# Which engine issues a transformer layer's first loads: eight token tiles from ScalarE's DMA queue instead of SyncE's

## The chip, the cores and the metric

The kernel runs on one core of a Trainium2 chip. Its engines are TensorE (PE for matrix products, PEld for the loads of their stationary operand), VectorE (DVE), ScalarE (ACT), GpSimd (POOL) and SyncE (SP). Each takes the instructions of its own queue in order, and they meet through semaphores. SP and ACT can both issue DMAs; the transfers run on 16 DMA engines. The metric is the device time of one execution, in microseconds (us). A measurement is the median of several runs.

## The reference

One layer of a hybrid backbone over 1024 latent tokens of 1024 channels, with 256 context tokens, in float32. What the change touches is the very beginning: modulation vectors from `c`, and a modulated RMS norm of the tokens that goes into the input projection.

```python
mod_x = (jax.nn.silu(c) @ w_mod[i] + b_mod[i])[:, None, :]
mod_c = (jax.nn.silu(c_ctx) @ w_mod[i] + b_mod[i])[None, None, :]
sh1, sc1, g1, sh2, sc2, g2 = jnp.split(mod_x, 6, axis=-1)
h = modulate(rms_norm(x, norm1_g[i]), sh1, sc1)      # h * (1 + scale) + shift
hc = modulate(rms_norm(ctx, norm1_g[i]), csh1, csc1)
proj = h @ w_in[i]
...
# S5 scans in both directions, pooling mixer, gated sum, output projection, residual
h2 = modulate(rms_norm(x, norm2_g[i]), sh2, sc2)
x = x + g2 * swiglu(h2, w_ffn_in[i], w_ffn_out[i])
return rms_norm(x, final_norm_g)
```

## The kernel before

The program is written out as one long sequence, and each engine's order is the order of the source. All products are float32 accuracy from split operands: each operand is divided into a high and a low part (ACT copies the high part, DVE subtracts), and three products are summed. `startup` is the first of the phases that `run` calls (lines 339 to 373); input projection, S5 states, gates, branches and the two feed-forward products come behind it.

`startup` (lines 474 to 728) loads and prepares the tokens:

- The tokens come as eight tiles of 128 tokens by 1024 channels, 512 KB each (`load_x`, line 482). The source is an access pattern of 8 by 16 rows of 1024 floats; the target `x3` holds all eight tiles side by side.
- Modulation needs the product of silu(c) with 2048 columns of `w_mod`, in four pairs of columns kp = 0 to 3 (shift and scale, 256 each). For every kp two loads of four rows of blocks come in (`load_mod(kp, i)`, line 489; each i is two DMAs of 512 KB into a buffer `wm`, of which there are three). `mod_rows(kp)` (line 537) multiplies both halves on PE and lets ACT copy the result, `mrow`; `mod_cols` (548) turns it into columns, with `b_mod` and `norm1_g` added on DVE from `self.cols`.
- Eight slabs of `w_in` of 192 KB (`load_slab`, line 499, three buffers) are split on ACT and DVE (`split_slab`). `slab(k)` splits slab k and loads slab k + 3.
- Per tile: a sum of squares (`squares`, ACT, one of them on DVE), a reciprocal root on DVE (`rstds`), a scaling (`scale`, on DVE and ACT by turns). Per block of channels: four transposes on PE (`trans`), the modulation on ACT and DVE (`mod`), and the products with a slab (`mm(kt, q)`, nine matmuls).

The calls at lines 587 to 725 set the order by hand. On SP stand the rows of `c` and `c_ctx` (`load_small`, line 391), two loads of modulation columns (four DMAs), the rows of `b_mod` and `norm1_g`, four tiles, two slabs, four tiles, more columns and slabs. On ACT stand the small loads of the S5 parameters (`s5_load_a`, line 877: `nat` twice and `ldt`, which DVE copies into `nat` at line 885). `self.cols[:, 0:16]` is silu of c and c_ctx (`columns(0)`, line 434), which DVE copies into `ccols` (line 607), the stationary operand of `mod_rows`.

The framework gives every DMA of SP and of ACT one of eight counting semaphores, DMAHW0 to DMAHW7, by turns in the order of the program. The order rows further down name them as waits.

Of the kernel before, what the change touches and what calls it, by code (L numbers as in the profile page):

```python
# [235 lines left out]
class Kernel:  # L236
# [237 lines left out]
    def startup(self, hs):  # L474
        nc = self.nc
        st = ExitStack()
        sp = st.enter_context(self.pool("startup", side="right"))
        self.hp = hs.enter_context(self.pool("h"))
        self.h = [self.hp.tile([128, 8, 1024], F32R, name=f"h{i}") for i in range(2)]
        x3 = sp.tile([128, 8, 1024], F32, name="x3")  # L480

        def load_x(t):
            src = bass.AP(tensor=self.x.tensor, offset=self.x.offset + t * D,
                          ap=[[8 * D, 8], [64 * D, 16], [1, D]])
            nc.sync.dma_start(x3[:, t], src)

        wm = {}

        def load_mod(kp, i):

            wm[kp, i] = sp.tile([128, 4, 2, 256], F32, name="wm", bufs=3)
            for s in range(2):
                c = s * D + kp * 256
                nc.sync.dma_start(wm[kp, i][:, :, s], self.w_mod[0, i * 512:i * 512 + 512, c:c + 256].rearrange(
                    "(k p) m -> p k m", p=128))
# [90 lines left out]

        self.rows = {}
        self.load_small(sp, 0)
        load_mod(0, 0)
        load_mod(0, 1)  # L590
        self.load_small(sp, 1)
        for t in range(4):
            load_x(t)
        load_slab(0)
        load_slab(1)
        for t in range(4, 8):
            load_x(t)
# [2 lines left out]
        self.constants()  # L600
        nc.scalar.activation(self.cols[:, 0:1], self.sgn, AF.Silu)
        self.window_sizes(sp)
        self.s5_load_a(sp)
        self.columns(0)
        ccols = sp.tile([128, 8, 32], F32, name="ccols")
        nc.gpsimd.memset(ccols, 0.0)
# [1487 lines left out]
```

## Time and profile before

| | us |
|---|---|
| median of 3 runs | 1327.31 |
| lowest and highest | 1327.28, 1331.72 |
| the profiled execution | 1331.82 |
| its span, first to last instruction | 1330.0 |

| engine | busy us | share of the span |
|---|---|---|
| PE | 1250.9 | 94% |
| PEld | 1006.5 | 76% |
| DVE | 952.6 | 72% |
| ACT | 520.7 | 39% |
| POOL | 11.1 | 1% |

The mean granted TensorE clock over the span was 0.981. In the views, a time that stands first in a row is counted from the start of the span. A row of the timeline is: start, duration, engine, line, operation, output <- input, number of instructions, and in brackets the idle time of the engine before it with what ended it. "ACTq" and "SPq" are those engines' instruction queues, where DMA issues stand; the duration of an issue isn't that of the transfer. The chain of waits is followed back from the last instruction: each piece is either work or the time until something landed. Idle time of an engine that isn't the bottleneck costs nothing by itself.

### The profile page before, as it was taken

What the parts mean: (1) busy time and instruction counts of PE and PEld (TensorE: products, weight loads), DVE (VectorE), ACT (ScalarE), POOL (GpSimd) and SP (SyncE); (2) the same over time, 40 slices, a digit from 0 to 9 for tenths busy, and PEclk for the clock granted to TensorE, in tenths of its full rate; (3) what the DMA queues carried; (4) which work ended last, traced back from release to release, by engine and by line L of the source; (5) the groups of instructions that cost most, each with busy time, mean ns of one, the idle gap of its engine ahead of it and who ended that gap; (6) DMA issues with size and microseconds to landing.
All of it is one profiled execution on the core that took longest, in us unless ns stands there. A gap on an engine that the chain in (4) does not pass through costs nothing.

```text
span 1330.0 us, 16713 instructions
## 1 busy us (share of the span) xinstructions
PE 1250.9 (94%) x5811; PEld 1006.5 (76%) x5811; DVE 952.6 (72%) x1802; ACT 520.7 (39%) x939; POOL 11.1 (1%) x36
## 2 busy tenths in 40 slices
PE   4898979999969999999998999999999999999995
PEld 3676757778867788788876788888888888888884
DVE  4679984799705686865678886687778766578576
ACT  3575213652215432232454333333333345454343
POOL 3000000000000000000000000000000000000000
PEclk8899999999989999999998999999999999999998
DMA  6834469226376565653513643676666538776543
GB/s 202 218 128 150 155 204 313 97 85 217 112 204 239 194 216 184 223 174 106 198 44 110 218 131 100 141 236 221 223 200 210 170 132 317 275 227 192 180 138 127
DMA packets 196108, 239.79 MB, mean 180 GB/s; under 512 B 16608, under 2 KB 117560, under 8 KB 195512
## 3 DMA queue, kind: packets, MB, share of 16 engines
q1 hardware_dynamic: 188168, 223.45, 52.9%
q10 hardware_dynamic: 7856, 15.27, 3.0%
q8 instruction: 46, 0.75, 0.2%
q14 instruction: 38, 0.31, 0.1%
HBM read 168.67 MB, written 70.00 MB: 179 GB/s over the span
## 4 chain that ended last, share of the span: by engine, by line
PE 59%; DVE 19%; DMA 10%; ACT 6%; issue 4%; SPq 2%; ACTq 0%; DVEq 0%
PE ps L1721 10%; PE ps L1723 10%; PE ps L1722 10%; PE ps L1952 5%; PE ps L1953 5%; PE ps L1951 5%; PE ps L264 3%; PE ps L268 3%; PE ps L266 3%; DMA x<-in_x_dram 2%; PE ps L1565 2%; PE ps L1567 2%; PE ps L1566 2%; DVE wt L98 1%; DVE V L1260 1%
## 5 line engine op out<-in xcount | busy, mean ns | idle before, releaser
L1721 PE MATMUL ps<-a,wt 128*128 128x512 f32 x436 | 173.6, 398 | 4.5 <-ACT ld L1835 4.2
L1723 PE MATMUL ps<-a,wt 128*128 128x512 f32 x436 | 172.2, 395 | 0.3 <-DVE wt L124 0.3
L1722 PE MATMUL ps<-a,wt 128*128 128x512 f32 x436 | 171.5, 393 | 0.0
L124 DVE TENSOR_TENSOR a<-a,a 128x512 fp32r<-128x512 f32 x162 | 103.3, 685 | 30.9 <-ACT a L225 30.4
L1952 PE MATMUL ps<-a,a 128*128 128x512 f32 x308 | 122.0, 396 | 1.1 <-DVE a L124 1.1
L1951 PE MATMUL ps<-a,a 128*128 128x512 f32 x308 | 121.8, 396 | 0.0
L1953 PE MATMUL ps<-a,a 128*128 128x512 f32 x308 | 121.8, 396 | 0.0
L264 PE MATMUL ps<-h,wt 128*128 128x512 f32 x336 | 109.9, 408 | 6.9 <-ACT wt L97 6.4
L268 PE MATMUL ps<-h,wt 128*128 128x512 f32 x336 | 105.8, 397 | 2.2 <-DVE wt L98 1.9
L266 PE MATMUL ps<-h,wt 128*128 128x512 f32 x336 | 105.5, 396 | 0.0
L225 ACT ACTIVATE a<-a 128x512 fp32r<-128x512 f32 x154 | 87.7, 624 | 43.3 <-DVE a L124 13.2
L1721 PEld LDWEIGHTS ps<-a,wt 128*128 128x128 f32 x436 | 82.4, 189 | 23.2 <-ACT ld L1835 4.6
L1723 PEld LDWEIGHTS ps<-a,wt 128*128 128x128 f32 x436 | 82.4, 189 | 20.7 <-DVE wt L124 1.2
L1722 PEld LDWEIGHTS ps<-a,wt 128*128 128x128 f32 x436 | 82.5, 189 | 18.6
L1365 ACT ACTIVATE a<-ld 128x512 fp32r<-128x512 f32 x64 | 39.3, 629 | 129.1 <-DVE ld L1542 64.6
L264 PEld LDWEIGHTS ps<-h,wt 128*128 128x128 f32 x336 | 60.7, 192 | 22.1 <-ACT wt L97 7.9
L268 PEld LDWEIGHTS ps<-h,wt 128*128 128x128 f32 x336 | 61.4, 191 | 16.8 <-DVE wt L98 4.7
L266 PEld LDWEIGHTS ps<-h,wt 128*128 128x128 f32 x336 | 62.0, 191 | 12.6
L98 DVE TENSOR_TENSOR wt<-raw,wt 128x1024 fp32r<-128x1024 f32 (+1 forms) x42 | 39.8, 950 | 42.6 <-ACT wt L97 42.5
L1952 PEld LDWEIGHTS ps<-a,a 128*128 128x128 f32 x308 | 57.9, 188 | 15.8 <-DVE a L124 1.9
L1951 PEld LDWEIGHTS ps<-a,a 128*128 128x128 f32 x308 | 57.9, 188 | 13.9
L1953 PEld LDWEIGHTS ps<-a,a 128*128 128x128 f32 x308 | 57.9, 188 | 13.8
(335 smaller groups left out, 2445.1 us busy)
## 6 DMA issues: line engine op xcount, KB each, us to landing
raw<-in_w_ffn_in_dram SPq DMA_DIRECT2D x44, 512.0 KB
ld<-in_w_mod_dram SPq DMA_DIRECT2D x64, 256.0 KB
a<-in_w_ffn_out_dram SPq DMA_DIRECT2D x55, 256.0 KB
raw<-in_w_in_dram SPq DMA_DIRECT2D x10, 1024.0 KB
wm<-in_w_mod_dram SPq DMA_DIRECT2D x16, 512.0 KB
ld<-in_w_ffn_out_dram SPq DMA_DIRECT2D x22, 256.0 KB
x<-in_x_dram SPq DMA_DIRECT2D x8, 512.0 KB
ETd<-out ACTq DMA_DIRECT2D x16, 256.0 KB
```

What stands on the lines that cost most here:

```text
L98: nc.vector.tensor_tensor(lo, src, hi.bitcast(F32), op=OP.subtract)
L124: self.K.nc.vector.tensor_tensor(lo, self.src, hi.bitcast(F32), op=OP.subtract)
L225: K.nc.scalar.activation(hi, t, AF.Copy)
L264: nc.tensor.matmul(o, wh, ah, start=first, stop=False)
L266: nc.tensor.matmul(o, wh, al, start=False, stop=False)
L268: nc.tensor.matmul(o, wl, ah, start=False, stop=last)
L1721: nc.tensor.matmul(p, wh, ah, start=first and k == 0, stop=False, skip_group_check=on)
L1722: nc.tensor.matmul(p, wh, al, start=False, stop=False, skip_group_check=on)
L1723: nc.tensor.matmul(p, wl, ah, start=False, stop=last and k == 3, skip_group_check=on)
L1951: nc.tensor.matmul(p, ah[:, s], wh, start=first and i == 0, stop=False, skip_group_check=on)
L1952: nc.tensor.matmul(p, ah[:, s], wl, start=False, stop=False, skip_group_check=on)
L1953: nc.tensor.matmul(p, al[:, s], wh, start=False, stop=i == NB - 1, skip_group_check=on)
```

## The change

`load_x` issues its DMA from ACT, and `s5_load_a` is called before the tiles' loads instead of after `window_sizes`.

```diff
@@ -482,7 +482,7 @@
         def load_x(t):
             src = bass.AP(tensor=self.x.tensor, offset=self.x.offset + t * D,
                           ap=[[8 * D, 8], [64 * D, 16], [1, D]])
-            nc.sync.dma_start(x3[:, t], src)
+            nc.scalar.dma_start(x3[:, t], src)
@@ -586,6 +586,7 @@
         self.rows = {}
         self.load_small(sp, 0)
+        self.s5_load_a(sp)
         load_mod(0, 0)
         load_mod(0, 1)
         self.load_small(sp, 1)
@@ -600,7 +601,6 @@
         self.constants()
         nc.scalar.activation(self.cols[:, 0:1], self.sgn, AF.Silu)
         self.window_sizes(sp)
-        self.s5_load_a(sp)
         self.columns(0)
```

ACT's queue from its start, before, with the counters that a row waits for (nat and ldt are the S5 parameters, cols the Silu of c, mrow the modulation row, x3 the tiles):

```order
L601 ACT_TABLE_LOAD
L601 ACTIVATE cols_317<-sgn_311 128x1 [waits DVE_49]
L882 DMA nat_341<-in_s5_a_re_dram 64x2x64
L882 DMA nat_341<-in_s5_a_im_dram 64x2x64
L884 DMA ldt_344<-in_s5_log_dt_dram 64x1
L441 ACTIVATE cols_317<-ps_347 128x16 [waits PE_49,Activation_49]
L546 ACTIVATE mrow_386<-ps_387 128x512 [waits PE_49]
L516 ACTIVATE h1_271,ss_273<-x3_272 128x1024 [waits DMAHW3_49]
```

The same place of ACT's queue in the changed kernel (line 602 is what was 601):

```order
L884 DMA ldt_281<-in_s5_log_dt_dram 64x1
L485 DMA x3_272<-in_x_dram 128x1x1024
L485 DMA x3_272<-in_x_dram 128x1x1024 [waits DMAHW0_49]
L485 DMA x3_272<-in_x_dram 128x1x1024 [waits DMAHW2_49]
L485 DMA x3_272<-in_x_dram 128x1x1024 [waits DMAHW4_49]
L485 DMA x3_272<-in_x_dram 128x1x1024 [waits DMAHW6_49]
L485 DMA x3_272<-in_x_dram 128x1x1024 [waits DMAHW0_49]
L485 DMA x3_272<-in_x_dram 128x1x1024 [waits DMAHW2_49]
L485 DMA x3_272<-in_x_dram 128x1x1024 [waits DMAHW4_49]
L602 ACT_TABLE_LOAD
L602 ACTIVATE cols_323<-sgn_317 128x1 [waits DVE_49]
L441 ACTIVATE cols_323<-ps_347 128x16 [waits PE_49,Activation_49]
```

The two loads of nat stand ahead of these rows, and all eight tiles now stand ahead of the table load. In the first turn of the counters nat has 0 and 2, ldt 4 and tile 0 has 6, so tiles 1 to 3 wait for nat, nat and ldt, and tiles 4 to 7 for tiles 0 to 3.

SP's queue at the same place in the changed kernel (wm are modulation columns, rows1 the rows of `b_mod` and `norm1_g`):

```order
L494 DMA wm_284<-in_w_mod_dram 128x4x256 x2
L494 DMA wm_287<-in_w_mod_dram 128x4x256 [waits DMAHW1_49]
L494 DMA wm_287<-in_w_mod_dram 128x4x256 [waits DMAHW3_49]
L400 DMA rows1_290<-in_b_mod_dram 48x128 [waits DMAHW5_49]
L400 DMA rows1_290<-in_norm1_g_dram 8x128 [waits DMAHW7_49]
L501 DMA slab_297<-in_w_in_dram 128x384 [waits DMAHW1_49]
L501 DMA slab_299<-in_w_in_dram 128x384 [waits DMAHW3_49]
L494 DMA wm_305<-in_w_mod_dram 128x4x256 [waits DMAHW5_49]
L494 DMA wm_305<-in_w_mod_dram 128x4x256 [waits DMAHW6_49]
```

Before, four tiles stood between rows1 and the slabs, and four behind them. The last row waits for counter 6, which tile 4 holds at that point. On DVE the copy of `ldt` (line 885) moves from behind `window_sizes` to the head of the queue. Nothing else moves on any engine, and from the second half of the second pair's columns on (`load_mod(1, 1)`) every DMA has the counter that it had before.

## Rows read from the trace of the kernel before

**Rows 1.** The page: span, and its chain that ended last, by engine.

```profile
span 1330.0 us, 16713 instructions
...
PE 59%; DVE 19%; DMA 10%; ACT 6%; issue 4%; SPq 2%; ACTq 0%; DVEq 0%
```

**Rows 2.** The chain of waits, 0 to 52 us: start, duration, what.

```profile
6.72 12.15 DMA x<-in_x_dram
...
18.89 20.10 DMA x<-in_x_dram
...
45.38 4.21 PE ps L579 x9
```

**Rows 3.** The timeline of ACT, 0 to 48 us.

```profile
0.71 1.28 ACT L601 ACT_TABLE_LOAD   x1 [0.71 <-PEq L2081]
...
3.28 0.18 ACT L441 ACTIVATE cols<-ps 128x16 f32<-128x16 f32 x1 [1.07 <-PE ps L437]
15.38 0.60 ACT L546 ACTIVATE mrow<-ps 128x512 f32<-128x512 f32 x1 [11.91 <-PE ps L543]
16.36 1.06 ACT L516 ACTIVATE h<-x 128x1024 fp32r<-128x1024 f32 x1 [0.39 <-DMA x<-in_x_dram]
...
24.81 1.06 ACT L516 ACTIVATE h<-x 128x1024 fp32r<-128x1024 f32 x1 [2.16 <-DMA x<-in_x_dram]
...
46.56 0.51 ACT L507 ACTIVATE wt<-slab 128x384 fp32r<-128x384 f32 x1
```

**Rows 4.** Waits of ACT, 0 to 48 us: total us, times, longest.

```profile
ACT h L516 <- DMA x<-in_x_dram: 10.0, 7, 2.5
```

**Rows 5.** SP's queue, 0 to 48 us: its waits, then issues of its timeline.

```profile
SPq L485 <- DMA x<-in_x_dram: 1.5, 2, 0.8
SPq L485 <- DMA ldt<-in_s_log_dt_dram: 1.3, 1, 1.3
...
5.90 3.96 SPq L485 DMA_DIRECT2D x<-in_x_dram  x4
```

**Rows 6.** Stretches: length, busy us by engine, granted clock, DMA share, GB/s.

```profile
2.60:6.00 3.40, 0.69 (x3) 0.43 (x3) 2.79 (x13) 0.18 (x1) 0.00 (x0) 1.00 0.97 287
...
14.00:22.00 8.00, 7.57 (x37) 6.16 (x30) 3.05 (x24) 3.39 (x6) 6.48 (x19) 1.00 0.55 204
22.00:26.00 4.00, 1.68 (x11) 1.44 (x10) 0.91 (x4) 1.84 (x5) 3.27 (x10) 1.00 0.84 199
29.00:32.00 3.00, 1.27 (x5) 0.98 (x6) 1.47 (x9) 2.43 (x4) 0.00 (x0) 0.50 0.89 229
...
44.00:50.00 6.00, 5.32 (x17) 3.35 (x19) 3.73 (x13) 3.00 (x5) 0.00 (x0) 0.50 0.24 73
```

**Rows 7.** The timelines of DVE and of PE, 0 to 56 us.

```profile
5.04 0.55 DVE L463 RECIPROCAL inv<-inv 128x64 f32<-128x64 f32 x1
8.64 0.22 DVE L885 COPY nat<-ldt 64x128 f32<-64x128 f32 x1 [3.05 <-DMA ldt<-in_s_log_dt_dram]
8.78 0.16 DVE L607 COPY ccols<-cols 128x16 f32<-128x16 f32 x1
...
9.21 1.93 PE L543 MATMUL ps<-wm,ccols 128*32 128x512 f32 x8
13.37 1.94 PE L543 MATMUL ps<-wm,ccols 128*32 128x512 f32 x8 [2.23 <-DMA wm<-in_w_mod_dram]
...
53.38 2.32 PE L579 MATMUL ps<-h,wt 128*128 128x512 f32 x9
```

**Rows 8.** ACT's issue; DMA queues (q1 SP, q10 ACT), 304.5 to 307.5, 308 to 310.5.

```profile
303.80 0.38 ACTq L1317 DMA_DIRECT2D sigb<-tmp  x1
...
q1 hardware_dynamic: 959, 1.12, 107.7%
...
q1 hardware_dynamic: 90, 0.70, 79.9%
q10 hardware_dynamic: 87, 0.18, 18.3%
```

## The prediction

> **What bounds the kernel now.** I read the page first: a span of 1330.0 us, with PE on 59% of the chain that ended last [rows 1]. A change that touches only the first loads can therefore matter only by moving the moment at which PE's long run of products begins. So I read the chain of waits over the first 52 us [rows 2]. It holds two long pieces of DMA, 12.15 us from the issue of the second token tile and 20.10 us from the issue of the eighth, which lands at 39.0. Behind it come squares, scales, transposes, the products of mm(0, 1) (4.21 us), and then mod_rows(1) and further issues on SP. From there on loads, PE, ACT and DVE follow each other in an order that the change leaves alone. I take as the **marker** the end of ACT's split of the third slab, 46.56 + 0.51 = 47.07 [rows 3]: SP's next issue behind it waits for that buffer, and the DMA queues are nearly idle until it comes (73 GB/s from 44 to 50 us [rows 6]). What the change does to the marker, it does to the end.
>
> ACT's timeline [rows 3] shows what leads there. ACT does its table load and two small Silus (done at 3.46), then waits for PE until 15.38 to copy the first modulation row (mrow, ends 15.98), then squares the tiles one by one. Its waits [rows 4] give 10.0 us over seven squares, each ended by a tile that landed. The tiles come slowly because they are alone on half of the engines: from 14 to 22 us the mean share of the sixteen is 0.55 at 204 GB/s, where 2.6 to 6 us, with modulation columns alone, has 0.97 at 287 GB/s [rows 6].
>
> **The change part by part.**
>
> *The rotation of semaphores.* The order rows show that all DMAs of both queues draw on eight counters, DMAHW0 to DMAHW7, in turn, and that a load waits until the one eight places earlier has landed. In the trace SP's issue of tiles waits for ldt's and an earlier tile's landing [rows 5]. After the change ACT holds these waits: tile 3 waits for ldt, and tiles 4 to 7 wait for tiles 0 to 3. ACT takes its instructions in order, so **nothing of ACT's work begins before tile 3 has landed and tile 7 is issued**: not the table load, not Silu of c, not the copy of mrow.
>
> *When tile 3 lands.* By then four modulation loads and four tiles must have moved, 8 x 0.52 = 4.2 MB, as before. Before, it landed where the fourth square starts, 24.8 [rows 3]. Now tiles and columns run beside each other. At 287 GB/s from 2.6 to 5 us, 0.7 MB goes; the other 3.5 MB at what the rows show when tiles and other loads mix, 199 to 229 GB/s [rows 6], takes 15.3 to 17.6 us. So tile 3 lands between 20.3 (best mix) and 24.8 (no gain at all); I take **22**, nearest to the mixed rows. ldt lands at 8.6 by the wait of its reader [rows 7] and doesn't decide.
>
> *What then stands behind it.* Issue of tile 7 about 0.65 (as an issue of SP's [rows 5]: four in 3.96 with waits in it, 0.6 to 1.0 each), table load 1.28, two Silus of 0.18 [rows 3], the copy into ccols 0.16 on DVE, both halves of mod_rows(0) on PE, 1.93 + 1.94 [rows 7], mrow 0.60 [rows 3], some 0.4 of hand-overs: 7.3 us. Before, all of it but the second half of mod_rows(0) was hidden under the loads. So mrow ends at 22 + 7.3 = **29.3, against 15.98**.
>
> *What comes off behind mrow.* From mrow's end to the marker there were 47.07 - 15.98 = 31.1 us. All eight tiles have landed or nearly so when they are wanted, so the 10.0 us of waits go [rows 4]: those of the first four (0.39 and 2.16 in [rows 3], two of 1.4 between them, 5.4 together) in full. Of the other 4.6 I count 2.2: when these squares come early, the reciprocal roots on DVE and the scaling are late next. That leaves 31.1 - 5.4 - 2.2 = 23.5 us, and the marker falls at 29.3 + 23.5 = 52.8, which is **5.7 us later**. Break-even is mrow at 23.6, that is tile 3 at 16.3.
>
> *The other edits.* s5_load_a moved up: its three loads now head ACT's queue, and the copy of ldt heads DVE's. DVE's constants (done at 5.59, some 4.8 us of work) wait for ldt until 8.6 [rows 7] and end near 13.5, still before ccols could be filled; cost nothing, cover 9 us. If that cover were gone, they would cost 5. The s5 terms on DVE and POOL move behind ccols by some 16 us; their next reader stands behind the marker; nothing. SP loses eight issues; slabs and the columns of the second pair wait for landings now and then, but are wanted only behind mrow; nothing. The work of PE, DVE and ACT is otherwise the same.
>
> [...]
>
> **The sum** against the profiled execution (1331.8 us, span 1330.0): + 5.7, so 1337.5. That execution is 4.5 above the median of the three runs, 1327.31, so the forecast is **1333.0**, slower by 0.43%. A measurement of this kernel can tell about 0.5% (6.6 us) from no change, so this counts as no change, close to the edge. The case itself reaches from + 2.1 (tile 3 at 20.3, clock regained) to + 8.5 (tile 3 at 24.8).
>
> [...] [Rows 8] show two queues meeting: a store of ACT's, issued at 303.80 while loads of SP's are under way, has no packet at all between 304.5 and 307.5 (q1, SP's queue, has all 959), and from 308 to 310.5 the queues move 87 (q10, ACT's) and 90 packets, one for one. [...]
>
> **The rivals.**
>
> *The columns starve (slower beyond the bound).* Packet for packet, as [rows 8] have it, a 4 KB row of a tile goes for each 1 KB row of modulation columns on the engines that they share. A modulation load is 512 rows, 32 on each engine, four loads 128. Some 18 of these go before the tiles begin near 5 us; the other 110 pass in pairs of 5 KB on eight engines: 110 x 8 x 5 KB = 4.5 MB at 204 GB/s = 22 us, so the fourth load lands near 27 or, at the 199 GB/s of the slowest mix [rows 6] and with the slabs' 0.4 MB between, near 30. Then the second half of mod_rows(0) and mrow (1.94 + 0.6 + 0.1) end at 29.7 to 32.6: + 6.1 to + 9.0. It decides over 0.5% when that load lands after 27.6. For it: the one-for-one row. Against it: the empty stretch before it, in which the later DMA of the other queue waited its turn. [...]
>
> *Tiles come early (no change, or a little faster).* If tiles take nearly all of their eight engines and the columns finish mostly on the other eight and in gaps, tile 3 could land at 5 + 2.1 MB / 204 GB/s = 15.3 to 18: marker - 1.0 to + 1.7, and with the clock regained - 2.9 at best: 1324.5 to 1329. Against it: x rows and column rows share engines, and in the stretches 22 to 26 and 29 to 32 the total hardly rises over the tiles' own 204 GB/s [rows 6].
>
> *ACT isn't held (faster).* If the issues don't hold ACT's work, mrow stays at 16 to 18 and some 7 us of the waits for tiles go: 1320. Against it: the order rows put all eight issues ahead of the table load, and in [rows 3] nothing of ACT runs out of order.
>
> *The change doesn't do what it says.* The queue isn't free of SP's: by the rotation a column load waits for tile 4, and tile 3 for ldt. That is in my sum.
>
> **How the numbers follow.** Forecast 0.60 (three tenths of it above + 6.6), columns starve 0.20, tiles early 0.15, ACT not held 0.05. Slower by over 0.5%: 0.18 + 0.20 = 0.38; within: 0.42 + 0.15 = 0.57; faster: 0.05. The range leaves out the faster case and the ends of the two neighbours: from - 1 to + 10, 1326 to 1338 us; it takes in both bounds of tile 3's landing, the clock, and the columns' worst.
>
> **What would show it.** ACT's timeline should have eight issues of tiles first, the last ending near 22.7, then the table load, and mrow ending near 29; the waits of squares for tiles should be almost gone; the third slab's split should end near 53, and everything behind 90 us look the same but later. Tile 3 landing by 17, a table load in the first microseconds, or mrow before 24 would prove the forecast wrong on the fast side; mod_rows(0) waiting for a modulation load past 27.6 means the columns starve. If the marker moves as said and the end doesn't, my claim that the start passes whole to the end is what failed.

## The result, and the profile after

| | before | changed |
|---|---|---|
| median, us | 1328.00 | 1341.34 |
| lowest and highest, 7 runs each | 1326.54, 1335.56 | 1335.32, 1346.69 |
| the profiled execution | 1331.82 | 1341.34 |
| its span | 1330.0 | 1339.5 |
| marker (end of the third slab's split) | 47.07 | 57.14 |

The changed kernel is **slower by 0.84%**: the ratio of its runs to those of before is 1.0084, with a 95% interval from 1.0064 to 1.0105. The forecast was + 0.43% and 1333.0 us, with a range to 1338; the time lies outside it.

The page of the changed kernel, its span and the chain by engine, against [rows 1]:

```profile
span 1339.5 us, 16708 instructions
...
PE 60%; DVE 19%; DMA 9%; ACT 7%; issue 4%; SPq 2%; ACTq 0%; DVEq 0%
```

The shares hardly differ: what changed is the start. The chain of waits there (start, duration, what), against [rows 2]:

```profile
7.61 18.78 DMA x<-in_x_dram
26.41 0.60 ACTq L485
27.13 1.20 issue
...
29.09 3.69 PE ps L543 x16
32.80 0.60 ACT mrow L546
...
55.45 2.33 PE ps L579 x9
```

One piece of DMA is left, the fourth tile (tile 3), issued at 7.61 and landed at 26.39. Behind it stand the issue of tile 7, the table load (the piece called issue), both halves of mod_rows(0) in one piece, and mrow, all on the chain. The timeline of ACT says the same, against [rows 3]:

```profile
2.82 24.19 ACTq L485 DMA_DIRECT2D x<-in_x_dram  x8
27.04 1.28 ACT L602 ACT_TABLE_LOAD   x1 [27.04 <-DMA x<-in_x_dram]
...
32.80 0.60 ACT L546 ACTIVATE mrow<-ps 128x512 f32<-128x512 f32 x1 [4.05 <-PE ps L543]
33.29 1.05 ACT L516 ACTIVATE h<-x 128x1024 fp32r<-128x1024 f32 x1
...
42.27 1.15 ACT L529 ACTIVATE x<-x,r2y 128x1024 f32<-128x1024 f32 x1 [1.80 <-DVE r2y L284]
...
56.63 0.51 ACT L507 ACTIVATE wt<-slab 128x384 fp32r<-128x384 f32 x1
```

Eight issues last from 2.82 to 27.01 and hold ACT; its first work begins at 27.04. The squares then follow each other without waiting for a tile, and the roots on DVE are late instead. In ACT's waits the row of [rows 4] is gone; these have come:

```profile
ACT L602 <- DMA x<-in_x_dram: 27.0, 1, 27.0
...
ACT x L529 <- DVE r6y L284: 1.8, 1, 1.8
ACT x L529 <- DVE r2y L284: 1.8, 1, 1.8
```

The transfers, by stretches as in [rows 6] (last three columns: clock, DMA share, GB/s), first the changed kernel:

```profile
8.00:12.00 4.00, 0.25 (x1) 0.06 (x1) 3.63 (x19) 0.00 (x0) 0.00 (x0) 1.00 1.00 194
12.00:18.00 6.00, 0.00 (x0) 0.00 (x0) 0.55 (x1) 0.00 (x0) 0.00 (x0) 1.00 0.51 156
18.00:26.00 8.00, 0.00 (x0) 0.00 (x0) 0.00 (x0) 0.00 (x0) 0.00 (x0) 1.00 0.56 168
```

and the kernel before, in two stretches that [rows 6] doesn't have:

```profile
12.00:18.00 6.00, 4.19 (x18) 2.36 (x19) 2.27 (x13) 1.75 (x3) 3.17 (x9) 1.00 0.61 202
24.00:26.00 2.00, 0.00 (x0) 0.00 (x0) 0.00 (x0) 1.19 (x3) 1.58 (x6) 1.00 0.85 173
```

With both queues at work from 8 to 26 us the changed kernel moves fewer bytes a second, 170 GB/s, than SP's queue alone did, 213. The DMA view from 12 to 18 us (queue: packets, MB, share) shows what they share:

```profile
q10 hardware_dynamic: 199, 0.75, 40.9%
q1 hardware_dynamic: 199, 0.19, 10.4%
```

ACT's tiles (q10) and SP's columns (q1) go packet for packet, 199 to 199. The fourth modulation load lands at 25.2 (13.3 before), and the tiles some 4 us apart, the last at 44.2 against 39.0. (A landing time, here and below, is the time of the last count that a load adds to its semaphore in the trace.)

### The profile page after: what moved, and what is told of

Its sections match the earlier page's. It is cut to its first block, busy times and chain, and to the rows that moved or that the text cites. A ratio compares the mean times of both kernels' runs of the same rounds, so it can differ in the third digit from the quotient of the medians.

```text
span 1339.5 us, 16708 instructions
## 1 busy us (share of the span) xinstructions
PE 1248.8 (93%) x5811; PEld 1005.8 (75%) x5811; DVE 953.6 (71%) x1802; ACT 519.8 (39%) x939; POOL 13.3 (1%) x36
## 4 chain that ended last, share of the span: by engine, by line
PE 60%; DVE 19%; DMA 9%; ACT 7%; issue 4%; SPq 2%; ACTq 0%; DVEq 0%
PE ps L1721 10%; PE ps L1723 10%; PE ps L1722 9%; PE ps L1952 5%; PE ps L1953 5%; PE ps L1951 5%; PE ps L268 3%; PE ps L264 3%; PE ps L266 3%; PE ps L1567 2%; PE ps L1565 2%; PE ps L1566 2%; DVE wt L98 1%; DMA x<-in_x_dram 1%; DVE V L1260 1%
## 5 line engine op out<-in xcount | busy, mean ns | idle before, releaser
L225 ACT ACTIVATE a<-a 128x512 fp32r<-128x512 f32 x154 | 87.3, 624 | 42.9 <-DVE a L124 13.2
L264 PEld LDWEIGHTS ps<-h,wt 128*128 128x128 f32 x336 | 60.7, 191 | 20.1 <-ACT wt L97 6.1
```

The lines of the kernel that those rows point to most:

```text
L225: K.nc.scalar.activation(hi, t, AF.Copy)
L264: nc.tensor.matmul(o, wh, ah, start=first, stop=False)
```

## The experiments

Where a kernel leaves work out or takes other tokens, its expectation says so. A table first, since one reading runs through all (its times, like every stretch below, come from one profiled execution of each kernel): how far the marker lies behind the landing of tile 7 and behind the end of the first mrow.

| kernel | tile 3 | tile 7 | mrow ends | marker | behind tile 7 | behind mrow | ratio to before (95%) |
|---|---|---|---|---|---|---|---|
| before | 24.7 | 39.0 | 15.98 | 47.07 | **8.1** | 31.1 | 1 |
| changed | 26.4 | 44.2 | 33.40 | 57.14 | 12.9 | **23.7** | 1.0084 (1.0064 to 1.0105) |
| e1_s5_only | 25.8 | 39.2 | 17.27 | 47.11 | **7.9** | 29.8 | 0.9998 (0.9985 to 1.0010) |
| e2_silu_first | 28.9 | 45.6 | 30.17 | 53.53 | **7.9** | **23.4** | 1.0048 (1.0031 to 1.0064) |
| e5_half_on_sp | 27.8 | 42.9 | 27.82 | 51.08 | **8.2** | **23.3** | 1.0025 (1.0005 to 1.0044) |
| e4_columns_later | 24.1 | 35.8 | 15.04 | 43.98 | **8.2** | 28.9 | 1.0000 (0.9984 to 1.0017) |
| e3_no_columns | 20.1 | 30.5 | 21.22 | 44.93 | 14.5 | **23.7** | one run |
| e6_sp_no_columns | 22.2 | 37.1 | 15.56 | 45.04 | **7.9** | 29.5 | one run |
| e12_pairs | 30.2 | 50.2 | 44.94 | 69.72 | 19.6 | **24.8** | 1.0134 (1.0098 to 1.0169) |
| e11_after_contig | 16.4 | 22.7 | 23.00 | 46.53 | 23.8 | **23.5** | 1.0004 (0.9988 to 1.0019) |
| e13_rows | 17.3 | 23.5 | 14.72 | 38.49 | 15.0 | **23.8** | 0.9930 (0.9912 to 0.9948) |
| e15_after_rows | 15.1 | 22.0 | 22.35 | 45.90 | 23.9 | **23.6** | 1.0012 (0.9996 to 1.0027) |

In every row the marker is the later of two: some 8 us behind tile 7, or 23.3 to 24.8 behind mrow. So the loss can have two causes, mrow's delay and tile 7's; in e2 and e5 both point at the same time. Three kernels that the table leaves out fit as well (e9 23.7 and e16 23.8 behind mrow, e14 7.9 behind tile 7); e7 and e8 don't, since there each tile waits for a whole group of loads.

### The hold of ACT: e1, e2, e5

**e1_s5_only**: the second edit alone.

```diff
         self.load_small(sp, 0)
+        self.s5_load_a(sp)
...
-        self.s5_load_a(sp)
```

> The kernel before with only the second edit: the S5 parameters are loaded ahead of the first modulation columns, the tiles stay with SP. My theory has it that the loss of the changed kernel comes from ACT being held behind its own tile issues and from tiles and columns sharing engines; this edit alone does neither. It expects mrow to end at 16 to 17 us, the marker (end of the third slab's split) at 46 to 49 us against 47.07, and a time within 2 us of the kernel before. The rival that the order of the S5 loads matters (DVE's constants wait for ldt, then ccols) expects ccols late, mrow at 18 or later, and 4 us or more of the loss of 11 to 13 us here already.

Measured: mrow 17.27, marker 47.11, ratio 0.9998. The S5 loads cost nothing, as the prediction had it.

**e2_silu_first**: the changed kernel with ACT's small work between the two groups of tiles.

```diff
         for t in range(4):
             load_x(t)
+        self.constants()
+        nc.scalar.activation(self.cols[:, 0:1], self.sgn, AF.Silu)
+        self.columns(0)
...
-        self.constants()
-        nc.scalar.activation(self.cols[:, 0:1], self.sgn, AF.Silu)
...
-        self.columns(0)
```

> The changed kernel, with the issues of tiles 4 to 7 moved behind the table load and the Silu work on ACT, so that the first modulation row no longer waits for tile 3; all transfers stay what they are. Theory of two parts (ACT held, and slow landing): mod_rows(0) then ends as soon as the fourth modulation load is there, 25.2 in the changed kernel, so mrow ends near 27.8 instead of 33.4, and the marker falls near 51.5 instead of 57.1: 5 to 6 us faster than the changed kernel, 4 to 5 slower than the kernel before (ratio to before near 1.0035). Rival that the hold costs nothing because the columns alone decide: fourth load still at 25.2, mrow no earlier than 32, time as the changed kernel (ratio 1.008). Rival that the hold is everything: mrow before 20 and a time as before or faster (ratio 1.000 or less).

Measured: mrow 30.17, marker 53.53, ratio 1.0048. The direction is right and the sizes aren't. ACT's timeline has

```profile
29.57 0.60 ACT L546 ACTIVATE mrow<-ps 128x512 f32<-128x512 f32 x1 [19.76 <-DMA x<-in_x_dram]
```

The product was ready, since the fourth modulation load had landed at 19.7; but ACT still stood in the issue of tile 7, which waits for tile 3, here at 28.9. The edit moved the hold and didn't take it away.

**e5_half_on_sp**: tiles 4 to 7 go back to SP, so that no issue of ACT waits for a tile.

```diff
-            nc.scalar.dma_start(x3[:, t], src)
+            (nc.scalar if t < 4 else nc.sync).dma_start(x3[:, t], src)
```

> The changed kernel with tiles 0 to 3 on ACT and tiles 4 to 7 back on SP, behind the two slabs. ACT then waits for nothing later than ldt (8 us), while tiles and columns still run beside each other. The runs so far have the marker 8.0 us behind the landing of tile 7 or 23.6 us behind the end of the first mrow, whichever is later. Theory of two parts: mrow follows the fourth modulation load (20 to 25 us) and ends at 22.5 to 28, tile 7 lands near 44 as in the changed kernel, the marker falls near 52, and the time is 5 us over the kernel before (ratio 1.0035), 5 to 6 under the changed kernel. Rival that the hold of ACT costs nothing: marker at 57, ratio 1.008. Rival that the hold is all of the loss: marker at 47, ratio 1.000.

Measured: mrow 27.82, tile 7 at 42.9, marker 51.08, ratio 1.0025. Chain of waits:

```profile
3.08 22.01 DMA wm<-in_w_mod_dram
```

mrow now follows the fourth modulation load, 25.1. Without the hold 6.1 us of the marker's 10.1 come back; the other 4.0 are late transfers. Not all of the 6.1 need be the hold: tile 7 lands 1.3 us sooner here than in the changed kernel, whose own tile 7 (44.2 + 8.1) would put the marker at 52.3, 4.8 before 57.14. So the hold costs 4.8 to 6.1. Both parts are real, and the two rivals, that the hold is nothing or all, fall.

### Is it the columns beside the tiles? e4, e3, e6, e12

**e4_columns_later**: the kernel before, without columns beside tiles 4 to 7.

```diff
-        load_mod(1, 0)
...
-        load_mod(1, 1)
...
         load_slab(3)
+        load_mod(1, 0)
+        load_mod(1, 1)
```

> The kernel before with one edit of SP's order: the two loads of the second pair of modulation columns are issued behind the fourth slab instead of between the fourth and fifth tile and behind the last tile. If tiles and columns that overlap slow each other, the later four tiles land some 2.6 us apart, the last near 35.5 instead of 39.0, the marker falls near 43.5 instead of 47.1, and the time is 2 to 4 us under the kernel before, as long as the second pair's columns still come before their product wants them. If sharing costs nothing beyond the bytes, the tiles gain less than 1.5 us; if the second pair becomes late, its product waits and the end is the same or later.

Measured: tile 7 at 35.8 and the marker at 43.98, as expected, but the ratio is 1.0000, within 2.2 us either way. At the second copy of cparts (ACT's work for the S5 states, line 922), some 35 us behind the marker, 2.4 of the 3.1 us are left (78.88 against 81.29). Whether they reach the end can't be told from these runs.

**e3_no_columns**: the changed kernel without the first two pairs' columns.

```diff
+            if kp < 2:
+                nc.gpsimd.memset(wm[kp, i], 0.0)
+                return
             for s in range(2):
```

> The changed kernel without the loads of the first two pairs of modulation columns; zeros written by POOL stand in their place, so the modulation vectors lack these columns. Nothing but small loads and the slabs then runs beside the tiles. If the tiles were slowed by columns on the same engines, they now land some 2.6 us apart (as the four that ran alone in the kernel before), tile 3 near 15 to 17 instead of 26.4 and tile 7 near 26 to 28 instead of 44.2, and ACT's table load starts near 16. If ACT's queue itself moves tiles more slowly than SP's, they still land about 4 us apart, tile 3 after 22.

**e6_sp_no_columns**: the same lines in the kernel before.

> The kernel before without the first two pairs of modulation columns (zeros by POOL in their place; the modulation vectors lack these columns), the tiles on SP: the counterpart of the run without columns that had its tiles on ACT. There tiles 0 to 3 landed at 10.7, 13.8, 17.4 and 20.1, some 3.1 us apart, and the later ones 2.6 apart. If ACT's queue is what made the first four slow, they land 2.6 us apart here, at 203 GB/s and more from 8 us on. If the start of a run of tiles is slow on any queue, they land some 3.1 us apart here too, at 160 to 170 GB/s. ACT isn't held, so mrow ends before 10 and the marker falls 8 us behind tile 7, near 38.

Both missed. First e3, then e6:

```profile
12.00:18.00 6.00, 0.82 (x4) 0.20 (x8) 0.95 (x5) 1.67 (x3) 0.00 (x0) 1.00 0.51 173
18.00:26.00 8.00, 7.02 (x53) 4.62 (x45) 6.95 (x43) 5.29 (x10) 5.34 (x10) 1.00 0.51 203
```

```profile
12.00:18.00 6.00, 5.57 (x28) 2.97 (x21) 4.41 (x25) 2.87 (x6) 3.38 (x6) 1.00 0.51 128
18.00:26.00 8.00, 4.66 (x29) 4.23 (x28) 4.03 (x30) 3.66 (x6) 6.66 (x18) 1.00 0.57 148
```

Tile 3 landed at 20.1 and at 22.2, not at 15 to 17. At the same share of 0.51 the tiles, with the engines nearly to themselves, ran at 203 in one stretch and at 128 in another, and SP's queue had the slower one. So ACT's queue alone isn't what makes them slow, and neither are the columns: **the loads of 8 by 16 rows have slow stretches of their own**.

**e12_pairs**: the tiles in four loads of two.

```diff
-                          ap=[[8 * D, 8], [64 * D, 16], [1, D]])
-            nc.scalar.dma_start(x3[:, t], src)
+                          ap=[[8 * D, 8], [64 * D, 16], [1, 2 * D]])
+            nc.scalar.dma_start(x3[:, t:t + 2].rearrange("p t d -> p (t d)"), src)
```

> The changed kernel with the eight tiles in four loads of two tiles (8 KB a row instead of 4 KB), all on ACT at the same place. With four loads the counters come round only as far as nat and ldt, so ACT is free at about 8.6 us: the hold is gone, the sharing of engines stays. If the queues share packet by packet, an 8 KB packet goes for each 1 KB of columns, the fourth modulation load lands at 30 or later, mrow ends after 32.5, and the marker falls near 57 as in the changed kernel (ratio 1.008). If they share by time or bytes, that load lands by 25, mrow ends by 28, the marker falls at 50 to 52, and the ratio is near 1.0025 as in the run with half of the tiles on SP.

Measured: the fourth modulation load lands at 42.2, mrow ends at 44.94, the marker is at 69.72, the ratio 1.0134. DMA view, 12 to 18 us:

```profile
q10 hardware_dynamic: 82, 0.66, 44.3%
q1 hardware_dynamic: 91, 0.09, 6.7%
```

The hold is gone and the kernel is slower still: an 8 KB packet goes for each small one of SP's. The queues share by packets here, not by bytes or time.

### What makes the tiles slow: e9, e11, e7, e8, e14, e16

**e9_alone_contig** (on e6) and **e11_after_contig** (on the changed kernel): tiles of consecutive rows.

```diff
-            src = bass.AP(tensor=self.x.tensor, offset=self.x.offset + t * D,
-                          ap=[[8 * D, 8], [64 * D, 16], [1, D]])
+            src = bass.AP(tensor=self.x.tensor, offset=self.x.offset + t * 128 * D,
+                          ap=[[16 * D, 8], [D, 16], [1, D]])
```

> The run without columns and with the tiles on SP once more, but each tile is now 128 consecutive rows of x (the eight engines read 64 KB apart, each its rows in sequence) instead of rows 32 KB apart between engines and 256 KB apart within one; the tokens come in another order, so the output is that of permuted tokens. In the run before it, tiles that had the DMA engines nearly to themselves landed 4.3 us apart at 117 to 139 GB/s, so it isn't columns that slow them there. If the addresses that the eight engines read at one time are the cause, the tiles land 2.6 us apart from the start, tile 3 near 15 and tile 7 near 26, at about 200 GB/s. If it is the writing side, or engines in step whatever they read, they land about 4 us apart again, tile 7 after 34.

> The changed kernel with tiles of 128 consecutive rows (output of permuted tokens); queues, waits and bytes as in the changed kernel. If the addresses read are what slows the mix of tiles and columns, the mix runs at 200 GB/s and more, tile 3 lands near 20 to 22 (the forecast's value) instead of 26.4, mrow ends near 27.5 to 29.5, the marker falls near 51 to 53, and the time is 4 to 6 us over the kernel before (ratio 1.003 to 1.005). If two queues that alternate packets are the cause whatever the addresses, tile 3 lands near 26 and the ratio is 1.008 again.

Measured from 8 to 12 us, in e9 and in e11:

```profile
8.00:12.00 4.00, 1.04 (x5) 0.38 (x9) 3.34 (x16) 0.00 (x0) 0.00 (x0) 1.00 1.04 375
```

```profile
8.00:12.00 4.00, 0.37 (x1) 0.18 (x1) 3.61 (x21) 0.00 (x0) 0.00 (x0) 1.00 1.04 400
```

Tiles land 1.3 us apart in e9 and 1.7 in e11, tile 7 at 17.0 and 22.7. That is faster than either theory had, because the premise was wrong: the load runs on all sixteen engines (share 1.04). As I read it, two dimensions of consecutive rows act as one of 128; no view shows that, but with a gap behind every 16 rows (e14, below) the share is 0.51 again. e11 shows what the change costs when tiles are fast: the hold is still there (mrow 23.0), and the ratio is 1.0004. Its tile 3 lands at 16.4, and the prediction's break-even was 16.3. But engines and addresses had both changed.

**e7_k16** (on the kernel before) and **e8_k16_later** (on e4): sixteen engines in another way.

```diff
         def load_x(t):
-            src = bass.AP(tensor=self.x.tensor, offset=self.x.offset + t * D,
-                          ap=[[8 * D, 8], [64 * D, 16], [1, D]])
-            nc.sync.dma_start(x3[:, t], src)
+            for i in range(8):
+                src = bass.AP(tensor=self.x.tensor, offset=self.x.offset + (8 * i + t) * D,
+                              ap=[[64 * D, 16], [1, 4 * D]])
+                nc.sync.dma_start(x3[16 * i:16 * i + 16, t:t + 4].rearrange("p t d -> p (t d)"), src)
```

> The kernel before with the tiles fetched in another shape: instead of eight loads of one tile, 8 by 16 rows, two groups of eight loads, each of 16 partitions and four tiles (16 contiguous KB a partition); all on SP, the order of everything else unchanged. If the tiles are slow because a load of 8 by 16 rows runs on eight engines, and 16 partitions run on sixteen, the share goes to about 1 in the stretch of tiles, tiles 0 to 3 land near 19 to 20 and tiles 4 to 7 near 27 instead of 39. The marker is then 23.6 behind mrow or the first tiles, near 42.5 to 43.5, and the time 3 to 5 us under the kernel before. If 16 partitions at a time are slower to write, the tiles gain nothing and the time is as before or longer, since tile 0 comes with tile 3.

> Both edits on the kernel before: tiles in two groups of eight loads of 16 partitions, and the second pair of modulation columns behind the fourth slab. Against the first of these edits alone only the columns move, and they no longer run beside tiles; tiles 4 to 7 land near 26, the marker is again near 42.5, and the time 3 to 6 us under the kernel before. If the second pair's product then waits for its columns, it ends 1 to 2 us later than with the first edit alone.

Both missed, with ratios of 1.0079 (1.0058 to 1.0100) and 1.0106 (1.0083 to 1.0129). e7:

```profile
12.00:18.00 6.00, 2.35 (x10) 0.52 (x10) 2.54 (x13) 0.60 (x1) 2.85 (x9) 1.00 0.96 152
```

All sixteen engines are busy and move 152 GB/s, in packets of 16 KB. The number of engines isn't enough.

**e14_alone_seq** (on e6): again 8 by 16 rows, consecutive within each group of 16.

```diff
-            src = bass.AP(tensor=self.x.tensor, offset=self.x.offset + t * D,
-                          ap=[[8 * D, 8], [64 * D, 16], [1, D]])
+            src = bass.AP(tensor=self.x.tensor, offset=self.x.offset + t * 120 * D,
+                          ap=[[17 * D, 8], [D, 16], [1, D]])
```

> The run without columns and with the tiles on SP, with rows that are consecutive within each engine but still eight by sixteen: engine i reads rows 17 i to 17 i + 15 of a block, so that the two dimensions don't merge and the load stays on eight engines (tokens partly repeated, output accordingly). If addresses made the tiles of the first such run slow (4.3 us apart, 280 ns a packet), they land 2.6 us apart at about 203 GB/s from the start, tile 3 near 14 and tile 7 near 25. If eight engines in step are slow whatever they read, they land about 4 us apart again.

```profile
12.00:18.00 6.00, 5.57 (x38) 2.96 (x31) 4.91 (x29) 2.97 (x6) 3.37 (x6) 1.00 0.51 141
```

Slow again, tile 3 at 21.4 against 22.2: this other order of addresses doesn't help. What the slow loads may have in common is the writing side: e7 (152 GB/s) writes 16 neighbouring partitions, and in the others eight engines write 16 apart, if each engine takes 16 neighbouring rows in turn. No view shows which engine reads or writes which rows; in the expectations of e9, e14 and e16 that is my supposition.

**e16_ports** (on e6): eight engines (share 0.51) that, by the same supposition, write 4 apart.

```diff
-            src = bass.AP(tensor=self.x.tensor, offset=self.x.offset + t * D,
-                          ap=[[8 * D, 8], [64 * D, 16], [1, D]])
-            nc.sync.dma_start(x3[:, t], src)
+            for q in range(4):
+                src = bass.AP(tensor=self.x.tensor, offset=self.x.offset + (4 * t + q) * 30 * D,
+                              ap=[[5 * D, 8], [D, 4], [1, D]])
+                nc.sync.dma_start(x3[32 * q:32 * q + 32, t], src)
```

> The run without columns and with the tiles on SP once more; each tile now comes in four loads of 32 neighbouring partitions, 8 by 4 rows, so that eight engines still do all the work in packets of 4 KB, but at one time they write partitions 4 apart instead of 16 apart (other rows of x, so other tokens, some twice). In the two runs on eight engines that wrote 16 apart, the stretch from 12 to 18 us had 203 and 222 packets at a share of 0.51, that is 0.51 x 16 x 6000 / 203 = 241 and 221 ns for each packet, the small ones included; in the kernel before the tiles run at about 160. If the partitions that the eight engines write at one time are the cause, the same count gives 160 to 175 ns here, at about 200 GB/s if the issues keep up. If eight engines are slow together whatever they write, it gives 215 ns or more again. [...]

Two stretches without slabs:

```profile
8.00:14.00 6.00, 3.04 (x17) 0.77 (x17) 5.10 (x25) 0.00 (x0) 0.72 (x1) 1.00 0.47 175
20.00:26.00 6.00, 4.03 (x24) 3.60 (x23) 5.20 (x23) 3.98 (x7) 5.07 (x13) 1.00 0.51 204
```

204 GB/s at a share of 0.51, where e6 and e14 had 128 and 141 from 12 to 18 us, and 140 and 172 at 0.52 from 20 to 26 (slabs among them); the earlier stretch falls short (share 0.47), which I put down to SP's issues, nine in its 6 us, though the later one has nine as well. At a full share that would be, as an estimate, 175 / 0.47 = 372 and 204 / 0.51 = 400 GB/s, against 128 / 0.51 = 251. (The stretch named in the expectation has two slabs in it, whose packets are shorter, 1.5 KB, and doesn't serve.) **That points to the partitions that the engines write at one time, and doesn't prove it.** e16 also cuts each tile into four smaller loads and reads rows 5 apart where e14 reads them 17 apart; and loads that by the same supposition write 16 apart reach 203 as well, in e3 from 18 to 26 us.

### A version that beats both, and the change under it: e13, e15

**e13_rows** (on the kernel before) and **e15_after_rows** (on the changed kernel): one dimension of 128 rows with a stride of eight, and the order of tokens restored where ACT reads the transposed block.

```diff
-                          ap=[[8 * D, 8], [64 * D, 16], [1, D]])
+                          ap=[[8 * D, 128], [1, D]])
...
-        nc.scalar.activation(tmp[:, :w], p[:, :w], AF.Identity, scale=m[:, 2 + z:3 + z], bias=m[:, z:z + 1])
+        src, to = p[:, :w], tmp[:, :w]
+        if rows:
+            src = src.rearrange("p (t j i) -> p t i j", j=16, i=8)
+            to = to.rearrange("p (t i j) -> p t i j", i=8, j=16)
+        nc.scalar.activation(to, src, AF.Identity, scale=m[:, 2 + z:3 + z], bias=m[:, z:z + 1])
```

> The kernel before with its tiles loaded as 128 rows with a stride of eight (one dimension of 128 instead of 8 by 16), which leaves the same tokens in each tile in another order of partitions; ACT's modulation reads the transposed block in the order that undoes it. Queues and order as before. Loads of consecutive rows ran on all sixteen engines at 350 to 420 GB/s and landed 1.3 us apart, but they changed two things, the number of engines and the addresses. If the number of engines is what counts, tiles land 1.3 to 1.5 us apart here too, tile 7 near 24 instead of 39, the marker is no longer set by tile 7 but lies 23.6 behind mrow, near 39.6, and the time is 5 to 7 us under the kernel before (ratio 0.995 to 0.996). If rows that lie a power of two apart are what is slow, whatever the number of engines, the tiles land 2.5 us or more apart, as in the run with 16 partitions a load (131 to 190 GB/s), and the ratio is 1.000 or more.

> The changed kernel (tiles on ACT, S5 loads early) with the same rows with a stride of eight and the same reading order. If these loads are fast, ACT is held only until tile 3 lands near 14 to 16 and mrow ends 7 us later, near 23; the marker lies 23.6 behind, near 46.5, 7 us later than in the kernel before with these loads and about where the kernel before has it: ratio to the kernel before near 1.000, to that kernel with the same loads near 1.005. If they are slow, the ratio is 1.008 or more.

e13, stretches:

```profile
12.00:18.00 6.00, 5.44 (x24) 3.61 (x25) 3.84 (x25) 3.81 (x7) 2.89 (x9) 1.00 1.03 404
```

and ACT's timeline:

```profile
14.12 0.60 ACT L550 ACTIVATE mrow<-ps 128x512 f32<-128x512 f32 x1 [10.65 <-PE ps L547]
...
37.98 0.51 ACT L511 ACTIVATE wt<-slab 128x384 fp32r<-128x384 f32 x1
```

The same rows of x, in another order, at 404 GB/s; tile 7 at 23.5, marker 38.49 (both within 1.2 us of the expectation), and a ratio of **0.9930 (0.9912 to 0.9948): 0.7% faster than the kernel before**, with one queue. Of the sixteen engines 8 by 16 rows had a share of 0.51 (e3, e6, e14), and 128 rows have 1.03; what decides it, no view shows.

Under these loads the change costs 1.0012 / 0.9930 = 1.0083. e15's chain of waits:

```profile
2.65 10.97 DMA wm<-in_w_mod_dram
13.64 6.14 DMA slab<-in_w_in_dram
19.78 1.95 PE ps L547 x8
21.75 0.61 ACT mrow L550
```

The second half of mod_rows(0) begins when the fourth modulation load is there, which lands at 19.6 (12.1 in e13) because tiles take turns with it: from 8 to 16 us ACT's queue moves 688 packets and SP's 684 (the view gives this wait to the slab issued behind it). ACT's hold (table load at 15.51) would let it begin only 0.3 us sooner, when the first half is done at 19.5. I had expected the hold alone; it is columns and hold at once, and mrow ends 7.6 us later than in e13.

## Why the prediction was wrong, step by step

**The step that failed is "When tile 3 lands".** It took 22, with bounds of 20.3 and 24.8; measured 26.39. Put into the same sum, 26.4 + 7.3 + 23.5 = 57.2, and the marker was 57.14. No other term is needed.

It failed in two places. The rate of 199 to 229 GB/s came from stretches of 3 and 4 us in [rows 6], as if it belonged to mixed traffic; the changed kernel ran at 156 and 168, and the last two microseconds of one of those stretches had shown 173. And the bound of 24.8, "no gain at all", held that transfers side by side can't take longer than one after the other. They can: from 8 to 26 us the kernel before moved 213 GB/s and the changed kernel 170.

The DMA view of the changed kernel from 12 to 18 us gives the price, as an estimate. A packet of ACT's took 0.409 x 16 x 6000 / 199 = 197 ns, and the packet of columns that goes for it 0.104 x 16 x 6000 / 199 = 50. A tile is 16 packets on each of eight engines: 16 x 247 = 4.0 us, the spacing seen, against 2.6 at the 203 GB/s of e3's fast stretch. Of the 1.4 us that each tile loses, 0.8 go to the columns between its packets and 0.6 to slower packets of its own. The first part is shown; what makes the tiles' own packets slow stays open.

What held:

- *The rotation of semaphores and the hold.* Eight issues first, the table load right behind the last. e5 prices it: 4.8 to 6.1 us of the marker.
- *What stands behind tile 3*: 7.3 forecast, 33.40 - 26.39 = 7.0 measured.
- *What comes off behind mrow*: 23.5 forecast, 57.14 - 33.40 = 23.74 measured, and 23.3 to 23.8 in six of the table's experiments. Within it, two items that I kept apart offset each other: the clock did come back (mm(0, 1) took 2.33 instead of the 4.21 of [rows 2], at a granted clock of 1.00 from 55.4 to 57.8 us instead of 0.50), and DVE's roots held ACT for 1.8 twice. The ends with the clock regained, + 2.1 and - 2.9, count up to 1.9 for it; 4.21 - 2.33 = 1.88 measured.
- *The other edits* cost nothing (e1).
- *The marker passes to the end*: + 10.1 at the marker, + 10.9 at the second copy of cparts, + 9.5 in the span. By the ratios it passes nearly whole in e2 (6.5 at the marker, 6.4 in the time), e5 (4.0 and 3.3) and e13 (8.6 and 9.3 less); e4's 3.1 doesn't show, and of e12's 22.7 some 17.8 are left.

The base was also low: the three runs shown had a median of 1327.31, larger sets of 7 to 23 runs of the same kernel 1328.0 to 1331.8. That is 0.7 to 4.5 us in the forecast's microseconds and nothing in its ratio, 1.0043 forecast and 1.0084 measured. The chances stood at 0.57 for no change and 0.38 for slower; the forecast's own case reached to + 8.5 at the marker, 1.6 us short.

The rivals. *Columns starve* asked for the fourth modulation load at 27 to 30; it came at 25.2 and decided nothing in the changed kernel, since ACT wasn't free. Its one-for-one count is nevertheless shown (199 to 199 from 12 to 18 us), and the fourth modulation load ends the wait for mrow in e5 and e12, and in e15 by 0.3 us. *Tiles early* came true only on sixteen engines (e11: tile 3 at 16.4, the marker 0.5 earlier than before, ratio 1.0004; that rival had 15.3 to 18 and - 1.0 to + 1.7). *ACT isn't held* didn't happen; and e5, which is that case made by hand, is not faster but 1.0025: without the hold a loss is left, if a small one.

What stays open: why the kernel before ran the very same loads at 202 GB/s, and e3 at 203 after 18 us. That the eight engines were out of step there, because the loads ahead of the tiles ended on each at another time, is a guess of mine and not shown. The traces speak against it being all: e6 from 31 to 34 us still starts its packets in bunches (slices of 0.075 us hold from 55 to 382 GB/s, e3's from 21 to 24 us 109 to 328) and yet moves 203 GB/s.

## What to carry to other kernels

Before moving loads to a queue of a compute engine, list what each issue waits for: here ACT took its queue in order, and its first work, at 27.04, stood behind the last of eight issues, which ended at 27.01. A forecast of transfers side by side needs a bound that is worse than one after the other (here 170 GB/s came, against 213 before), and a rate that holds in every part of the stretches it is read from (one of 199 had a half at 173). And look first at the shape of the load: here the stride of one access pattern was worth 0.7%, while changing its queue lost 0.8%.

## What the runs showed of the hardware that was not expected

- Loads of 8 by 16 rows moved 128, 141 or 173 GB/s in some stretches and 203 in another, with little beside them and at the same share of 0.51 (e6, e14, e3); loads of 8 by 4 rows 204 (e16).
- Loads to 16 neighbouring partitions moved 152 GB/s at a share of 0.96 (e7), and one-dimensional loads to 128 partitions 404 at 1.03 (e13).
- Two queues moved about as many packets as each other in both sizes tried: 4 KB against 1 KB, 199 to 199; 8 KB against mostly 1 KB, 82 to 91.
